# A rotary embedding on one core: six of eight rows of a tile worked in pairs, and the last tile stored as one transfer

## The chip, the cores and the metric

The kernel runs on one core of a Trainium2 chip. The metric is the device time of one execution in microseconds (us). Most executions of one kernel agree within 0.3%, so a difference of a tenth of a microsecond means nothing here. A run is called fast when it is not over 1.5% above the fastest of its kernel. Engines: PE is TensorE, PEld its weight loads, DVE VectorE, ACT ScalarE, POOL GpSimd, SP SyncE, whose queue issues all large transfers. In a profile page, a row of 40 digits gives the busy tenths of 40 equal slices of the span (9 is 90% or more), and the line of a DMA queue gives its packets, the MB moved and the share of the time of 16 DMA engines. The "span" is the profiled stretch of one execution; the device time is some 1.7 to 1.9 us longer.

## The reference

`x` has shape (16, 512, 1024) in fp32. Each row of 1024 is 16 heads of 64. Every head is split in halves `x1` and `x2` and rotated by tables that depend on the position in the sequence:

```python
x1, x2 = x[..., :half_dim], x[..., half_dim:]
rotated = concatenate([x1 * cos - x2 * sin, x1 * sin + x2 * cos], axis=-1)
```

So out = x * cos + swapped(x) * (-sin, sin): two products and one sum for each element, while 33.6 MB have to be read and as much written.

## The kernel before

The input is cut into 8 tiles of 128 partitions x 8 rows x 1024 numbers (4.2 MB each). The kernel keeps five tiles on the chip. The queue loads five tiles, stores tiles 0 to 2, loads tiles 5 to 7 into their places, and stores the rest. The results overwrite the tile.

```python
FIRST = (3, 8)        # tile 0 is loaded in two pieces
LAST_OUT = (4, 8)     # the last tile is stored in two halves
...
for t in range(NT):
    for k in range(KK):                       # eight rows of a tile
        r = xt[:, k * dim : (k + 1) * dim]
        own = k in DVE_B[t % 2]               # row 0
        if not own:                           # seven sine products on GpSimd
            b = bp.tile([P, dim], FP32, name="b")
            nc.gpsimd.tensor_tensor(out=halves(b), in0=swapped(r, nh), in1=over_heads(sk), op=ALU.mult)
        if k in PE_ROWS[t % 2]:               # rows 0 and 4: summed by TensorE, copied by ScalarE
            ...
        else:                                 # six rows: product and sum on VectorE
            add(1)
            ps = pd.tile([P, dim], FP32, name="pd")
            nc.vector.tensor_tensor(out=pairs(ps), in0=pairs(r), in1=cos_b(k, 2 * nh), op=ALU.mult)
            pending.append((r, ps, b))        # later: r = ps + b on VectorE
    ...
def finish(t):
    add(0)
    for hi in LAST_OUT if t == NT - 1 else (KK,):
        store(t, lo, hi)
```

## Time and profile before

| | before |
|---|---|
| device time | 162.39 us, median of 3 (162.34 to 162.41) |
| span | 160.7 us |
| VectorE busy | 141.4 us (88%) |
| GpSimd busy | 130.3 us (81%) |
| share of the DMA engines | 97.9% |
| moved | 67.24 MB, 432 GB/s from 10 to 150 us |

The prediction below shows the lines and reads them.

### The profile page before, as it was taken

The numbers are of one execution on the slowest core, as the hardware profiler recorded it, in microseconds if no ns is written. First come the engines' busy times: TensorE is split into PE (matmuls) and PEld (weight loads), VectorE is DVE, ScalarE is ACT, GpSimd is POOL, SyncE is SP. The second block draws the span as 40 slices with busy tenths as digits, with TensorE's granted clock in tenths as the row PEclk, the third lists the DMA queues.
The fourth block names the chain that finished last, engine by engine and source line by source line (L and its number), as shares of the span: only waits on it lengthen the run. The fifth ranks groups of instructions, "written<-read, shape, count | busy, mean of one in ns | idle before, by whom it ended". The sixth has DMA issues, their size and how long they took to land. (4 is left out here: it accounts for less than half of the span.)

```text
span 160.7 us, 531 instructions
## 1 busy us (share of the span) xinstructions
PE 62.1 (39%) x71; PEld 20.0 (12%) x71; DVE 141.4 (88%) x142; ACT 20.0 (12%) x33; POOL 130.3 (81%) x62
## 2 busy tenths in 40 slices
PE   3146370536217250709045540918063722735000
PEld 0112010202011110202020200211020201120000
DVE  1059999999999999999999999999999999999800
ACT  0201120021102020111102020202001110202000
POOL 1039999999999999999999899999999799940000
PEclk9999958576956776595555555555555585587655
DMA  5999999999999999999999999999999999999994
GB/s 190 398 408 473 392 490 424 392 481 432 392 432 473 394 432 473 400 400 498 408 400 465 441 400 434 457 416 424 465 408 424 473 408 416 465 416 412 416 432 192
DMA packets 2852, 67.26 MB, mean 419 GB/s; under 512 B 418, under 2 KB 546, under 8 KB 546
## 3 DMA queue, kind: packets, MB, share of 16 engines
q1 hardware_dynamic: 2752, 67.24, 97.9%
q10 hardware_dynamic: 98, 0.00, 0.0%
q14 instruction: 2, 0.02, 0.0%
HBM read 33.69 MB, written 33.55 MB: 419 GB/s over the span
## 5 line engine op out<-in xcount | busy, mean ns | idle before, releaser
L168 POOL TENSOR_TENSOR b<-xt,sns 128x1024 f32<-128x1024 f32 x56 | 129.6, 2354 | 11.6 <-DVE sns L111 9.2
L186 DVE TENSOR_TENSOR pd<-xt,tab 128x1024 f32<-128x1024 f32 x48 | 58.1, 1225 | 0.8
L148 DVE TENSOR_TENSOR xt<-pd,b 128x1024 f32<-128x1024 f32 x48 | 58.3, 1217 | 0.0
L181 PE MATMUL ps<-xt,ident 128*128 128x512 f32 x32 | 29.6, 1082 | 49.0 <-issue 38.4
L181 PE MATMUL ps<-b,ident 128*128 128x512 f32 x32 | 29.0, 1061 | 29.6 <-DVE ps L174 27.0
L182 ACT COPY xt<-ps 128x512 f32<-128x512 f32 x32 | 18.7, 585 | 120.4 <-PE ps L181 120.4
L174 DVE TENSOR_TENSOR ps<-xt,tab 128x512 f32<-128x512 f32 x32 | 20.6, 687 | 0.0
L181 PEld LDWEIGHTS ps<-xt,ident 128*128 128x128 f32 x32 | 9.4, 324 | 68.3 <-issue 63.7
L181 PEld LDWEIGHTS ps<-b,ident 128*128 128x128 f32 x32 | 9.2, 316 | 49.6 <-issue 25.6
L179 DVE TENSOR_TENSOR xt<-xt,tab 128x1024 f32<-128x1024 f32 x8 | 9.8, 1221 | 0.4
L110 DVE TENSOR_SCALAR sns<-tab 128x256 f32<-128x256 f32 x1 | 0.4, 425 | 8.1 <-PE tab L108 8.1
L107 PE MATMUL tab<-b,spread 64*128 64x256 f32 x2 | 1.2, 697 | 5.0 <-DMA b<-in_sin_dram 5.0
L182 ACT ACT_TABLE_LOAD x1 | 1.3, 1283 | 7.1 <-DMA xt<-in_x_dram 7.1
L97 PE MATMUL ps<-zero 128*128 128x512 bf16 x3 | 1.5, 623 | 1.2 <-DVE zero L94 1.2
L107 PEld LDWEIGHTS tab<-b,spread 64*128 64x128 f32 x2 | 0.5, 306 | 5.9 <-issue 5.9
L108 PE MATMUL tab<-b,spread 64*128 64x256 f32 x2 | 1.1, 632 | 0.0
L94 DVE MEMSET zero<- 128x256 uint32 x1 | 0.3, 272 | 0.9 <-PEq L211 0.9
L108 PEld LDWEIGHTS tab<-b,spread 64*128 64x128 f32 x2 | 0.7, 334 | 0.2
L106 DVE COPY spread<-ident 64x64 f32<-64x64 f32 x2 | 0.3, 182 | 0.2 <-POOL ident masks.py:199 0.2
L97 PEld LDWEIGHTS <-zero 128*128 128x128 bf16 x3 | 0.3, 124 | 1.5 <-DVE zero L94 1.2
masks.py:197 POOL MEMSET ident<- 128x128 f32 x1 | 0.2, 204 | 0.3 <-POOLq L211 0.3
L111 DVE COPY sns<-tab 128x256 f32<-128x256 f32 x1 | 0.4, 414 | 0.0
(6 smaller groups left out, 0.9 us busy)
## 6 DMA issues: line engine op xcount, KB each, us to landing
xt<-in_x_dram SPq DMA_DIRECT2D x7, 4096.0 KB, 29.1
out_dram<-xt SPq DMA_DIRECT2D x7, 4096.0 KB, 27.8
out_dram<-xt SPq DMA_DIRECT2D x2, 2048.0 KB, 8.4
xt<-in_x_dram SPq DMA_DIRECT2D x1, 2560.0 KB
xt<-in_x_dram SPq DMA_DIRECT2D x1, 1536.0 KB, 6.3
b<-in_sin_dram SPq DMA_DIRECT2D x1, 64.0 KB, 6.3
b<-in_cos_dram SPq DMA_DIRECT2D x1, 64.0 KB, 6.1
spare<-in_sin_dram ACTq DMA_DIRECT2D x1, 0.9 KB, 5.7
```

What stands on the lines that cost most here:

```text
L97: nc.tensor.matmul(out=ps, lhsT=zero[:, :P], rhs=zero, start=True, stop=True)
L107: nc.tensor.matmul(out=sin_t, lhsT=spread, rhs=sin_sb, start=True, stop=True)
L108: nc.tensor.matmul(out=cos_t, lhsT=spread, rhs=cos_sb, start=True, stop=True)
L110: nc.vector.tensor_scalar_mul(out=sns[:, :, 0, :], in0=sin_k, scalar1=-1.0)
L111: nc.vector.tensor_copy(out=sns[:, :, 1, :], in_=sin_k)
L148: nc.vector.tensor_tensor(out=r, in0=ps, in1=b, op=ALU.add)
L168: nc.gpsimd.tensor_tensor(out=halves(b), in0=swapped(r, nh), in1=over_heads(sk), op=ALU.mult)
L174: nc.vector.tensor_tensor(out=pairs(ps), in0=pairs(rc), in1=cos_b(k, BANK // half), op=ALU.mult)
L179: nc.vector.tensor_tensor(out=halves(r), in0=halves(r), in1=swapped_signed(k), op=ALU.mult)
L181: nc.tensor.matmul(out=ps, lhsT=ident, rhs=rhs, start=False, stop=True, skip_group_check=True)
L182: nc.scalar.copy(out=rc, in_=ps)
L186: nc.vector.tensor_tensor(out=pairs(ps), in0=pairs(r), in1=cos_b(k, 2 * nh), op=ALU.mult)
```

## The change

The intent is to save VectorE and GpSimd the fixed cost of instructions: six of the eight rows go in pairs, with one product and one sum of 2048 elements instead of two of 1024. Since the computation should then end earlier, the last tile is stored in one piece. Row 0 and row 3 (formerly 4) remain the ones that TensorE sums. The products of pairs have one buffer in PSUM (an on-chip memory) instead of two, and some tiny transfers differ as well.

```diff
-PE_ROWS = ((0, 4), (0, 4))
-DVE_B = ((0,), (0,))
+ROW_OWN, ROW_PE = 0, 3
+PAIRS = ((1, 2), (4, 5), (6, 7))
-LAST_OUT = (4, 8)
+LAST_OUT = (8,)
-SMALL = (15, 14, 12, 8)
+EXTRA = 5
...
-    bp = ctx.enter_context(tc.tile_pool(name="bp", bufs=B_BUFS))     # 6 of 1024
+    bp = ctx.enter_context(tc.tile_pool(name="bp", bufs=3))          # 3 of 2048
...
-    pd = ctx.enter_context(tc.tile_pool(name="pd", bufs=2, space=bass.MemoryType.PSUM))
+    pd = ctx.enter_context(tc.tile_pool(name="pd", bufs=1, space=bass.MemoryType.PSUM))
...
+    def pair_product(t, k):
+        ps = pd.tile([P, 2 * dim], FP32, name="pd")
+        cos_product(ps, rows(t, k, 2), k, 2)
+        return ps, rows(t, k, 2)
+    def pair_sum(ps, r, b):
+        nc.vector.tensor_tensor(out=r, in0=ps, in1=b, op=ALU.add)
...
+    for t in range(NT):
+        b1 = sin_rows(t, first[0], 2)        # GpSimd
+        p1 = pair_product(t, first[0])       # VectorE
+        own_product(r0)
+        ...
+        b3 = sin_rows(t, ROW_PE, 1)
+        b2 = sin_rows(t, second[0], 2)
+        pair_sum(*p1, b1)
+        pe_half(ROW_PE, *h0)
+        p2 = pair_product(t, second[0])
+        b1 = sin_rows(t, third[0], 2)
+        pair_sum(*p2, b2)
+        pe_half(ROW_PE, *h1)
+        p1 = pair_product(t, third[0])
+        if t + 1 < NT:
+            cos_product(own_ps, rows(t + 1, ROW_OWN), ROW_OWN)
+        pair_sum(*p1, b1)
+        stores(t)
```

(`+        ...` stands for TensorE's sum of row 0.)

More of the change, by code (lines that the diff above doesn't have):

```diff
@@ L14 @@
 BUFS = 5
-B_BUFS = 6
 BANK = 512
-PE_ROWS = ((0, 4), (0, 4))
-DVE_B = ((0,), (0,))
+ROW_OWN, ROW_PE = 0, 3
+PAIRS = ((1, 2), (4, 5), (6, 7))
 FIRST = (3, 8)
-LAST_OUT = (4, 8)
-SMALL = (15, 14, 12, 8)
+LAST_OUT = (8,)
+EXTRA = 5
 @with_exitstack
@@ L61 @@
     xp = ctx.enter_context(tc.tile_pool(name="xp", bufs=BUFS))
-    bp = ctx.enter_context(tc.tile_pool(name="bp", bufs=B_BUFS))
+    bp = ctx.enter_context(tc.tile_pool(name="bp", bufs=3))
     pfix = ctx.enter_context(tc.tile_pool(name="pfix", bufs=1, space=bass.MemoryType.PSUM))
-    pe = ctx.enter_context(tc.tile_pool(name="pe", bufs=3, space=bass.MemoryType.PSUM))
-    pd = ctx.enter_context(tc.tile_pool(name="pd", bufs=2, space=bass.MemoryType.PSUM))
+    pe = ctx.enter_context(tc.tile_pool(name="pe", bufs=1, space=bass.MemoryType.PSUM))
+    pd = ctx.enter_context(tc.tile_pool(name="pd", bufs=1, space=bass.MemoryType.PSUM))
     ctx.enter_context(tc.manual_schedule())
@@ L81 @@
     load(0, 0, FIRST[0])
-    sin_sb = bp.tile([P, dim], FP32, name="b")[:PB, : KK * half]
-    cos_sb = bp.tile([P, dim], FP32, name="b")[:PB, : KK * half]
+    tabs = bp.tile([P, 2 * dim], FP32, name="b")
+    sin_sb = tabs[:PB, : KK * half]
+    cos_sb = tabs[:PB, dim : dim + KK * half]
     nc.sync.dma_start(out=sin_sb, in_=sin_v)
@@ L89 @@
         load(t)
+    spare = fixed.tile([1, EXTRA, 16], FP32)
+    for i in range(EXTRA):
+        nc.sync.dma_start(out=spare[:1, i], in_=sin_v[:1, :16])
     ident = fixed.tile([P, P], FP32)
@@ L94 @@
     nc.vector.memset(zero, 0.0)
-    for i in range(3):
-        ps = pe.tile([P, BANK], FP32, name="ps")
+    own_ps = pe.tile([P, dim], FP32)
+    pe_ps = pe.tile([P, BANK], FP32)
+    for ps in (own_ps[:, :BANK], own_ps[:, BANK:], pe_ps):
         nc.tensor.matmul(out=ps, lhsT=zero[:, :P], rhs=zero, start=True, stop=True)
-    spare = fixed.tile([16, len(SMALL), 16], FP32)
     sns = fixed.tile([P, KK, 2, half], FP32)
@@ L104 @@
     spread = fixed.tile([PB, P], FP32)
-    for b in range(NB):
-        nc.vector.tensor_copy(out=spread[:, b * PB : (b + 1) * PB], in_=ident[:PB, :PB])
+    eye = ident[:PB, :PB]
+    nc.vector.tensor_copy(
+        out=spread.rearrange("p (b q) -> p b q", b=NB),
+        in_=bass.AP(tensor=eye.tensor, offset=eye.offset, ap=[eye.ap[0], [0, NB], [1, PB]]),
+    )
     nc.tensor.matmul(out=sin_t, lhsT=spread, rhs=sin_sb, start=True, stop=True)
@@ L111 @@
     nc.vector.tensor_copy(out=sns[:, :, 1, :], in_=sin_k)
-    on_dve = sorted(set(DVE_B[0]) | set(DVE_B[1]))
-    sns_t = tab[:, KK * half : KK * half + len(on_dve) * hd]
-    for i, k in enumerate(on_dve):
-        nc.vector.tensor_copy(out=sns_t[:, i * hd : (i + 1) * hd], in_=sns[:, k])
-    def cos_b(k, n):
-        c = cos_t[:, k * half : (k + 1) * half]
-        return bass.AP(tensor=c.tensor, offset=c.offset, ap=[c.ap[0], [0, n], [1, half]])
-    def over_heads(s):
-        return bass.AP(tensor=s.tensor, offset=s.offset, ap=[s.ap[0], [0, nh], [1, hd]])
@@ L124, in swapped @@
-    def swapped(r, n):
-        return bass.AP(
-            tensor=r.tensor, offset=r.offset + half, ap=[r.ap[0], [hd, n], [-half, 2], [1, half]]
-        )
-    def swapped_signed(k):
-        i = on_dve.index(k)
-        s = sns_t[:, i * hd : (i + 1) * hd]
-        return bass.AP(
-            tensor=s.tensor, offset=s.offset + half, ap=[s.ap[0], [0, nh], [-half, 2], [1, half]]
-        )
-    def pairs(r):
-        return r.rearrange("p (a j) -> p a j", j=half)
-    def halves(r):
-        return r.rearrange("p (h a j) -> p h a j", a=2, j=half)
@@ L143, with heads, swapped @@
-    pending = []
-    def add(most):
-        while len(pending) > most:
-            r, ps, b = pending.pop(0)
-            nc.vector.tensor_tensor(out=r, in0=ps, in1=b, op=ALU.add)
-    def finish(t):
-        add(0)
+    own_t = tab[:, KK * half : KK * half + hd]
+    nc.vector.tensor_copy(out=own_t, in_=sns[:, ROW_OWN])
+    def heads(r):
+        return r.rearrange("p (h a j) -> p h a j", a=2, j=half)
+    def swapped(r):
+        n = r.shape[1] // hd
+        return bass.AP(tensor=r.tensor, offset=r.offset + half, ap=[r.ap[0], [hd, n], [-half, 2], [1, half]])
@@ new lines, in rows, with cos_product @@
+    def rows(t, k, n=1):
+        return tiles[t][:, k * dim : (k + n) * dim]
+    def cos_product(out, r, k, n=1):
+        c = cos_t[:, k * half : (k + n) * half]
+        m = r.shape[1] // (n * half)
+        if n == 1:
+            cb = bass.AP(tensor=c.tensor, offset=c.offset, ap=[c.ap[0], [0, m], [1, half]])
+            o, i = (z.rearrange("p (a j) -> p a j", j=half) for z in (out, r))
+        else:
+            cb = bass.AP(tensor=c.tensor, offset=c.offset, ap=[c.ap[0], [half, n], [0, m], [1, half]])
+            o, i = (z.rearrange("p (k a j) -> p k a j", k=n, j=half) for z in (out, r))
+        nc.vector.tensor_tensor(out=o, in0=i, in1=cb, op=ALU.mult)
@@ new lines, in own_product, with sin_product @@
+    def own_product(r):
+        s = bass.AP(
+            tensor=own_t.tensor,
+            offset=own_t.offset + half,
+            ap=[own_t.ap[0], [0, nh], [-half, 2], [1, half]],
+        )
+        nc.vector.tensor_tensor(out=heads(r), in0=heads(r), in1=s, op=ALU.mult)
+    def sin_product(out, r, k, n):
+        s = sns[:, k : k + n].rearrange("p k a j -> p (k a j)")
+        if n == 1:
+            sb = bass.AP(tensor=s.tensor, offset=s.offset, ap=[s.ap[0], [0, nh], [1, hd]])
+            o, i = heads(out), swapped(r)
+        else:
+            sb = bass.AP(tensor=s.tensor, offset=s.offset, ap=[s.ap[0], [hd, n], [0, nh], [1, hd]])
+            o = out.rearrange("p (k h a j) -> p k h a j", k=n, a=2, j=half)
+            i = bass.AP(
+                tensor=r.tensor,
+                offset=r.offset + half,
+                ap=[r.ap[0], [dim, n], [hd, nh], [-half, 2], [1, half]],
+            )
+        nc.gpsimd.tensor_tensor(out=o, in0=i, in1=sb, op=ALU.mult)
@@ new lines, in sin_rows, with parts, pe_add, pe_half @@
+    def sin_rows(t, k, n):
+        b = bp.tile([P, 2 * dim], FP32, name="b")[:, : n * dim]
+        sin_product(b, rows(t, k, n), k, n)
+        return b
+    def parts(r):
+        return [r[:, i * BANK : (i + 1) * BANK] for i in range(r.shape[1] // BANK)]
+    def pe_add(ps, other):
+        nc.tensor.matmul(out=ps, lhsT=ident, rhs=other, start=False, stop=True, skip_group_check=True)
+    def pe_half(k, r, b):
+        cos_product(pe_ps, r, k)
+        pe_add(pe_ps, b)
+        nc.scalar.copy(out=r, in_=pe_ps)
@@ L152, in finish, with stores @@
+    def pair_product(t, k):
[4 more added lines that the diff above has]
+        nc.vector.tensor_tensor(out=r, in0=ps, in1=b, op=ALU.add)
+    def stores(t):
         lo = 0
@@ L158, in finish @@
                 load(n)
+    cos_product(own_ps, rows(0, ROW_OWN), ROW_OWN)
     for t in range(NT):
-        xt = tiles[t]
-        for k in range(KK):
-            r = xt[:, k * dim : (k + 1) * dim]
-            own = k in DVE_B[t % 2]
-            if not own:
-                b = bp.tile([P, dim], FP32, name="b")
-                sk = sns[:, k].rearrange("p a j -> p (a j)")
-                nc.gpsimd.tensor_tensor(out=halves(b), in0=swapped(r, nh), in1=over_heads(sk), op=ALU.mult)
-            if k in PE_ROWS[t % 2]:
-                parts = []
-                for c in range(0, dim, BANK):
-                    ps = pe.tile([P, BANK], FP32, name="ps")
-                    rc = r[:, c : c + BANK]
-                    nc.vector.tensor_tensor(
-                        out=pairs(ps), in0=pairs(rc), in1=cos_b(k, BANK // half), op=ALU.mult
-                    )
-                    parts.append((ps, rc, swapped(rc, BANK // hd) if own else b[:, c : c + BANK]))
-                if own:
-                    nc.vector.tensor_tensor(out=halves(r), in0=halves(r), in1=swapped_signed(k), op=ALU.mult)
-                for ps, rc, rhs in parts:
-                    nc.tensor.matmul(out=ps, lhsT=ident, rhs=rhs, start=False, stop=True, skip_group_check=True)
-                    nc.scalar.copy(out=rc, in_=ps)
-            else:
-                add(1)
-                ps = pd.tile([P, dim], FP32, name="pd")
-                nc.vector.tensor_tensor(out=pairs(ps), in0=pairs(r), in1=cos_b(k, 2 * nh), op=ALU.mult)
-                pending.append((r, ps, b))
-            if k == 0 and t > 0:
-                finish(t - 1)
-            add(1)
@@ L191 @@
-        if t == NT // 2 - 1:
-            for i, n in enumerate(SMALL):
-                nc.scalar.dma_start(out=spare[:n, i], in_=sin_v[:n, :16])
-    finish(NT - 1)
+        first, second, third = PAIRS
+        b1 = sin_rows(t, first[0], 2)
+        p1 = pair_product(t, first[0])
+        r0 = rows(t, ROW_OWN)
+        own_product(r0)
+        for ps, r in zip(parts(own_ps), parts(r0)):
+            pe_add(ps, swapped(r))
+        nc.scalar.copy(out=r0, in_=own_ps)
+        b3 = sin_rows(t, ROW_PE, 1)
@@ L198 @@
+        b2 = sin_rows(t, second[0], 2)
+        pair_sum(*p1, b1)
+        h0, h1 = zip(parts(rows(t, ROW_PE)), parts(b3))
+        pe_half(ROW_PE, *h0)
[8 more added lines that the diff above has]
+        stores(t)
 _INS = ['x', 'cos', 'sin', 'num_heads']
```

## The prediction

> **What bounds the kernel now.** I read first the page's busy shares and slices, then the table of DMA queues.
>
> ```profile
> PE 62.1 (39%) x71; PEld 20.0 (12%) x71; DVE 141.4 (88%) x142; ACT 20.0 (12%) x33; POOL 130.3 (81%) x62
> ...
> DVE  1059999999999999999999999999999999999800
> ACT  0201120021102020111102020202001110202000
> POOL 1039999999999999999999899999999799940000
> ...
> DMA  5999999999999999999999999999999999999994
> ...
> q1 hardware_dynamic: 2752, 67.24, 97.9%
> ```
>
> Three resources look full: VectorE (DVE), GpSimd (POOL) and the 16 DMA engines. What tells them apart is the edges. VectorE is idle in the first two slices and stops two slices before the end; the DMA row is full from the second slice to the last but one. The queue row says the same: 97.9% of 16 engines' span. So transfers bound the kernel, and VectorE matters only through when it releases stores. Next I cut the trace into windows (columns after the length: busy time of PE, PEld, DVE, ACT, POOL, then granted clock, DMA share, GB/s).
>
> ```profile
> 10.00:150.00 140.00, 58.64 (x64) 18.57 (x64) 138.68 (x138) 18.73 (x32) 129.60 (x56) 0.65 1.00 432
> 157.00:157.50 0.50, 0.00 (x0) 0.00 (x0) 0.00 (x0) 0.00 (x0) 0.00 (x0) 0.50 0.84 360
> 157.50:158.00 0.50, 0.00 (x0) 0.00 (x0) 0.00 (x0) 0.00 (x0) 0.00 (x0) 0.50 0.92 393
> 158.00:158.50 0.50, 0.00 (x0) 0.00 (x0) 0.00 (x0) 0.00 (x0) 0.00 (x0) 0.50 0.77 328
> 158.50:159.00 0.50, 0.00 (x0) 0.00 (x0) 0.00 (x0) 0.00 (x0) 0.00 (x0) 0.50 0.16 66
> ```
>
> From 10 to 150 us the DMA share is 1.00 at 432 GB/s: no hole. So a 4096 KB tile (4.194 MB) takes 4.194/432 = 9.7 us, and the engines run dry at about 158.5 us, the last of them a little later. Then the timeline of the end, and of the queue's own issues:
>
> ```profile
> 0.73 0.38 SPq L75 DMA_DIRECT2D xt<-in_x_dram  x1
> ...
> 147.14 1.22 DVE L148 TENSOR_TENSOR xt<-pd,b 128x1024 f32<-128x1024 f32 x1
> 148.39 1.23 DVE L186 TENSOR_TENSOR pd<-xt,tab 128x1024 f32<-128x1024 f32 x1
> 149.53 2.35 DVE L148 TENSOR_TENSOR xt<-pd,b 128x1024 f32<-128x1024 f32 x2
> ...
> 146.04 6.25 SPq L79 DMA_DIRECT2D out_dram<-xt  x2
> ```
>
> Computation ends at 149.53 + 2.35 = 151.88 us, the last half tile's store is issued at once (the issues end at 146.04 + 6.25 = 152.29), and its 2.1 MB need 4.9 us of the engines. Since they run dry at 158.5, they had earlier work until 153.6: the last half store joined a queue that was not yet empty. Today VectorE is some 1.6 us early at the only place where it could matter. The chain of waits ends in VectorE work, but that is the order of releases, not the limit.
>
> **What the Trainium skill says.**
> 1. "VectorE: DVE Perf Modes", section on the TRN2 errata: an fp32 tensor_tensor of N elements takes (N+151)/0.96 ns, exact at 512 and 2048. That is 691 and 1224 ns for 512 and 1024; the trace has 687, and 1217 to 1225. It agrees, so I use 2.29 us at 2048.
> 2. "GPSIMD Engine Reference", 3.1: a tensor_tensor of 2048 fp32 elements took 4497 ns. The trace shows only 1024 elements, 2354 ns; two of those are 4.71, so the pair would save 0.2 us of fixed cost. I use 4.5.
> 3. "DMA: Bandwidth & Descriptors", latency: about 0.6 us to the first byte for transfers issued by SyncE. This trace shows more: first load issued at 0.73 us, nothing moved before 1.7. I use 1.0.
> 4. "Perfetto Trace Analysis", DMA Optimizations: splitting a transfer lets parts start sooner. The change undoes such a split, so that is the part to fear.
>
> **The change part by part.**
>
> The lines for the operations concerned:
>
> ```profile
> L168 POOL TENSOR_TENSOR b<-xt,sns 128x1024 f32<-128x1024 f32 x56 | 129.6, 2354 | 11.6 <-DVE sns L111 9.2
> L186 DVE TENSOR_TENSOR pd<-xt,tab 128x1024 f32<-128x1024 f32 x48 | 58.1, 1225 | 0.8
> L148 DVE TENSOR_TENSOR xt<-pd,b 128x1024 f32<-128x1024 f32 x48 | 58.3, 1217 | 0.0
> ...
> L174 DVE TENSOR_TENSOR ps<-xt,tab 128x512 f32<-128x512 f32 x32 | 20.6, 687 | 0.0
> ...
> L179 DVE TENSOR_TENSOR xt<-xt,tab 128x1024 f32<-128x1024 f32 x8 | 9.8, 1221 | 0.4
> ```
>
> *VectorE.* A tile has 17 instructions now (6 + 6 + 4 + 1) and 10 afterwards: three products and three sums of 2048, two products of 512, and two of 1024. Elements stay equal: 15 x 1024. What counts is start to start. The timeline gives 149.53 - 148.39 = 1.14 us behind an instruction whose result is not awaited, and 148.39 - 147.14 = 1.25 behind one that is. With 1024 more elements at 1/0.96 ns: 2.20 and 2.32. For 512 it is 0.60. Afterwards a tile has two direct dependences (the second sum on its product, the next tile's first product on the one product buffer): 6 x 2.20 + 2 x 1.14 + 2 x 0.60 + 2 x 0.11 = 16.9 us. Now it is (151.88 - 10.75)/8 = 17.6. Saved: 0.7 us a tile.
>
> *GpSimd.* Per tile three of 4.5 and one of 2.35: 15.9 us, below VectorE's 16.9; now seven times 2.35 less overlap. It stays second, except in the first tile. There GpSimd starts at 10.54 and delivers the first pair at 15.0, the single row at 17.4 and the second pair at 21.9. VectorE from 10.75: 1.14 + 2.20 + 1.14 = 15.2, sum 17.4, half row 18.0, product 20.2; then it waits 1.7 us for the second pair. Sum 24.1, half row 24.7, product 26.9, next tile's first product 28.1, sum 30.3. GpSimd's third pair is there at 26.4, and its lead grows afterwards. The three buffers of b are freed in time: the third pair reuses the first pair's, free at 17.4.
>
> *End of computation.* 30.3 + 7 x 16.9 - 1.1 (no next tile) = 147.5 us, against 151.9 now. So 4.4 us earlier, all beside the transfers.
>
> *The last store.* It is now 9.7 us of transfer issued at once. The engines have nothing else from 158.5 - 9.7 = 148.8 us on. To reach them in time it has to be issued by 148.8 - 1.0 = 147.8. It is issued at about 147.5 to 147.6. So the early end of computation is spent, nearly to the last tenth, on the coarser store. The latest engine has a little more slack than the mean one, and it is the latest that sets the end.
>
> *The rest.* The order of large transfers is the same. Store 0 moreover waits for load 2 (a shared DMA semaphore). Five loads occupy the engines to about 52 us, and load 2 has landed by about 34, so nothing runs dry. The five tiny transfers replace four tiny ones (49 rows); the latter have 0.0% of the queue table. PE and ACT have the same matmuls and elements, and the own row's copy is one of 1024; both are idle over half the time.
>
> Sum: transfers unchanged, expected bubble before the last store 0 to 0.3 us. Time 162.4 plus 0.1: **162.5 us**.
>
> **Rivals.**
> A. *The coarse last store opens a hole.* For it: the margin above is 0.3 us out of an estimate over eight tiles; 0.1 us a tile of error moves it by 0.8. Against it: 512, 1024 and the skill's 2048 lie on one line. If VectorE were as slow as now, the issue would be at 151.9, 4.1 us late: 166.5 us (slower by 2.5%). With half the saving: about 164.5.
> B. *GpSimd becomes the bound.* For it: the pair product walks one dimension more, and GpSimd has under 1.1 us of slack a tile. Against it: its present product already swaps halves and runs steadily at 2342 to 2368 ns. At 5% more it just matches VectorE; at 15% more, 18.3 us a tile, computation would end near 157 and the time be 171 or so.
> C. *The saved VectorE work shows in the time.* For it: VectorE is 88% busy and lies on the chain of waits. Against it: the 1.00 DMA share from 10 to 150 us. It would need DMA holes, and there are none; were it true, 4.4 us less: 158.
> D. *Two transfers' worth of smoother DMA*, fewer and larger packets at the end or other tiny transfers: some tenths either way.
>
> **Range and chances.** My centre has no hole or a small one. The upper end allows 1.2 us of hole, the lower end some tenths of better DMA: 162.0 to 163.6. Slower by 2% means over 165.6, a hole of 3.2 us, possible only if A is nearly whole or B is true: 0.05. Faster needs C: 0.01. Within 2%: 0.94.
>
> **What would show it.** In the profile afterwards: DMA share about 98% and the same GB/s; VectorE instructions of 2048 at 2.28 to 2.30 us, GpSimd's at 4.45 to 4.6; VectorE waiting for GpSimd some 1.7 us in tile 0 and hardly later; computation ending near 147.5; the last store issued then and landing about 12 us later; DMA share under 1 for at most some tenths around 148 to 149. Wrong would be: pair instructions longer than twice the single ones, GpSimd busy without pause and VectorE waiting in each tile, or a hole in the DMA row before the last store.

## The result, and the profile after

The changed kernel took 162.38 us (median of 4, 162.19 to 162.47), the kernel before in the same rounds 162.40 us (162.34 to 162.44). The ratio is 0.9997, 95% interval 0.998 to 1.0015: the same. A ratio here is always the mean time of one kernel's fast runs over that of the other's fast runs of the same rounds, so it is not quite the ratio of the medians.

The page of the changed kernel, the lines that answer to those shown of before:

```profile
PE 56.4 (35%) x71; PEld 18.8 (12%) x71; DVE 136.3 (85%) x85; ACT 18.1 (11%) x25; POOL 127.2 (79%) x38
...
DVE  1059969999999999999999999999999999998000
POOL 1049999999999999988998899898999899840000
...
DMA  5999999999999999999999999999999999999993
...
q1 hardware_dynamic: 2618, 67.24, 97.9%
```

VectorE has 57 instructions fewer and 5.1 us less busy time, and its row ends one slice (4 us) earlier. The DMA row and the queue's 97.9% have not moved. From 10 to 150 us the windows give 432 GB/s in both kernels. The large transfers are the same, and so is the time.

The groups by shape (busy us and mean ns of one, then the idle time before them and who ended it) show the costs of the paired instructions:

```profile
L165 POOL TENSOR_TENSOR b<-xt,sns 128x2048 f32<-128x2048 f32 x24 | 108.4, 4530 | 14.5 <-DVE sns L117 9.1 <-DVE xt L189 5.4
L141 DVE TENSOR_TENSOR pd<-xt,tab 128x2048 f32<-128x2048 f32 x24 | 55.0, 2291 | 0.2
L189 DVE TENSOR_TENSOR xt<-pd,b 128x2048 f32<-128x2048 f32 x24 | 54.9, 2287 | 2.4 <-POOL b L165 1.6
```

A pair costs VectorE 2.29 us, where two single instructions cost 2 x 1.22 = 2.44, and GpSimd 4.53, where two cost 4.71. VectorE waits for GpSimd once, 1.6 us in the first tile; GpSimd waits 5.4 us in all for VectorE to free buffers. So GpSimd is the second of the two, not the first.

The end of the computation in the timeline (start, duration), and the issue of the last store:

```profile
138.21 2.29 DVE L141 TENSOR_TENSOR pd<-xt,tab 128x2048 f32<-128x2048 f32 x1
...
140.60 2.29 DVE L189 TENSOR_TENSOR xt<-pd,b 128x2048 f32<-128x2048 f32 x1
...
143.40 2.29 DVE L141 TENSOR_TENSOR pd<-xt,tab 128x2048 f32<-128x2048 f32 x1
...
145.80 2.29 DVE L189 TENSOR_TENSOR xt<-pd,b 128x2048 f32<-128x2048 f32 x1
...
148.15 0.33 SPq L78 DMA_DIRECT2D out_dram<-xt  x1
```

VectorE ends at 148.09 us instead of 151.88, so 3.8 us earlier. The single store leaves at 148.15 us. In the packet records of this run, ten of the sixteen DMA engines have a hole of 0.08 to 0.55 us at about 149 us, before the first packet of the last store; the others had earlier work until then. Fifteen engines end between 158.74 and 158.99 us. The sixteenth has no hole and ends at 159.51: it was late anyway, and it is the one that the end waits for. In the kernel before, the ends lie between 158.32 and 159.38. The early end of computation has thus been spent on the coarser store.

### The profile page after: what moved, and what is told of

Same layout as the page of the kernel before. It is cut to its first block, busy times and chain, and to the rows that moved or that the text cites. A ratio compares the mean times of both kernels' runs of the same rounds, so it can differ in the third digit from the quotient of the medians.

```text
span 160.7 us, 443 instructions
## 1 busy us (share of the span) xinstructions
PE 56.4 (35%) x71; PEld 18.8 (12%) x71; DVE 136.3 (85%) x85; ACT 18.1 (11%) x25; POOL 127.2 (79%) x38
## 3 DMA queue, kind: packets, MB, share of 16 engines
q1 hardware_dynamic: 2618, 67.24, 97.9%
## 4 chain that ended last, share of the span: by engine, by line
DVE 68%; issue 12%; POOL 6%; DMA 4%; PE 1%; SPq 0%; DVEq 0%
DVE xt L189 33%; DVE pd L141 31%; POOL b L165 6%; DMA b<-in_sin_dram 4%; DVE pe_ps L141 3%; PE tab L113 1%; PE tab L114 1%; DVE sns L116 0%; DVE xt L150 0%; DVE own_ps L141 0%; SPq L74 0%; DVE sns L117 0%; DVEq L189 0%
## 5 line engine op out<-in xcount | busy, mean ns | idle before, releaser
L165 POOL TENSOR_TENSOR b<-xt,sns 128x2048 f32<-128x2048 f32 (+1 forms) x32 | 126.5, 3987 | 14.5 <-DVE sns L117 9.1
L189 DVE TENSOR_TENSOR xt<-pd,b 128x2048 f32<-128x2048 f32 x24 | 54.9, 2287 | 2.4 <-POOL b L165 1.6
L141 DVE TENSOR_TENSOR pd<-xt,tab 128x2048 f32<-128x2048 f32 x24 | 55.0, 2291 | 0.2
L176 PE MATMUL own_ps<-xt,ident 128*128 128x512 f32 x32 | 29.1, 1064 | 54.0 <-DVE xt L150 48.3
L176 PE MATMUL pe_ps<-b,ident 128*128 128x512 f32 x32 | 25.2, 880 | 29.1 <-DVE pe_ps L141 29.1
L176 PEld LDWEIGHTS own_ps<-xt,ident 128*128 128x128 f32 x32 | 9.4, 324 | 74.0 <-DVE xt L150 59.3
L209 ACT COPY xt<-own_ps 128x1024 f32<-128x1024 f32 x8 | 8.1, 1013 | 72.2 <-PE own_ps L176 72.2
L181 ACT COPY xt<-pe_ps 128x512 f32<-128x512 f32 x16 | 9.4, 589 | 40.7 <-PE pe_ps L176 40.7
L141 DVE TENSOR_TENSOR pe_ps<-xt,tab 128x512 f32<-128x512 f32 x16 | 11.0, 686 | 0.0
L141 DVE TENSOR_TENSOR own_ps<-xt,tab 128x1024 f32<-128x1024 f32 x8 | 9.8, 1223 | 0.0
```

The lines of the kernel that those rows point to most:

```text
L141: nc.vector.tensor_tensor(out=o, in0=i, in1=cb, op=ALU.mult)
L165: nc.gpsimd.tensor_tensor(out=o, in0=i, in1=sb, op=ALU.mult)
L176: nc.tensor.matmul(out=ps, lhsT=ident, rhs=other, start=False, stop=True, skip_group_check=True)
L181: nc.scalar.copy(out=r, in_=pe_ps)
L189: nc.vector.tensor_tensor(out=r, in0=ps, in1=b, op=ALU.add)
L209: nc.scalar.copy(out=r0, in_=own_ps)
```

## Experiments

My theory: the DMA engines set the time. The computation has only to release the last store before the queue runs dry, the single store moved that deadline 4 to 5 us forward, and the pairs moved the computation forward by nearly as much. The rivals: the pairs do gain time and the single store eats exactly that (so undoing the store should show 158.5 us); the single store costs nothing by itself; VectorE or the computation's traffic still governs the time.

Each experiment is an edit of the changed kernel unless it says otherwise. Results are correct except in the one without computation. Each kernel before in these rounds had a median of 162.34 to 162.38 us.

### The four combinations

**The changed kernel again**, as a yardstick.

> The changed kernel once more, as the yardstick beside the next three on the same chip. Theory (the DMA engines set the time, the computation only has to release the last store by about 148 us): 162.2 to 162.5 us, ratio to the kernel before within 0.2% of 1; computation ends at 148.1 and most engines have a hole of 0.1 to 0.6 us before the last store, hidden behind the one engine that is latest anyway. Rival (VectorE's shorter work shows in the time and something else takes it back): no different time, so this run alone does not tell them apart.

Measured: 162.37 us (162.25 to 162.46, 5 runs), ratio 0.9998 (0.9985 to 1.0012). VectorE ended at 147.88 us in its profile, and holes stood on five engines only (0.07 to 0.29 us). The latest engine again had no hole and ended at 159.41. As expected.

**Pairs, with the last store in halves again.**

```diff
-LAST_OUT = (8,)
+LAST_OUT = (4, 8)
```

> Pairs as in the change, but the last tile stored in two halves as before. Theory: the holes of 0.1 to 0.6 us at 149 us vanish (the second half is needed only at about 152.8 and is issued at 148.2), but the time moves by no more than 0.3 us: 162.1 to 162.4, same. Rival (the pairs gain 4 us and the single store costs 4 us, so they cancel): with the split store back, the gain shows, about 158.5 us.

Measured: 162.52 us (162.16 to 162.61, 5 runs), ratio 1.0004 (0.9991 to 1.0016). The gain that the rival wanted, 4 us, does not appear, although VectorE ends at 148.55 us and nothing is coarse any more. The median lies 0.1 us above the stated 162.1 to 162.4, which is within the scatter. The packet records show no hole on any engine around the last store, as expected. The pairs by themselves are worth nothing here. ("Pairs" stands for all of the change but the last store, the tiny transfers included; these were not tested apart.)

**Single rows, with the last store in one piece** (an edit of the kernel before).

```diff
-LAST_OUT = (4, 8)
+LAST_OUT = (8,)
```

> Single rows as in the kernel before, but the last tile stored as one transfer. Theory: the store is issued at 151.9 to 152.0, its first bytes move 1.0 us later, at 152.9, while the engines have run dry between 148.6 and 149.7; so a hole of 3 to 4 us on each of them, no more hidden by the latest one, and 165.7 to 166.3 us (slower by 2.0 to 2.4%). Rival (a store of one piece costs nothing, as it is hidden anyway): 162.4.

Measured: 165.88 us (165.65 to 166.04, 4 runs), ratio 1.0214 (1.02 to 1.0228): 3.5 us slower. VectorE ends at 152.19. The queue's timeline and the windows (length, busy time by engine, clock, then DMA share and GB/s):

```profile
152.26 0.33 SPq L79 DMA_DIRECT2D out_dram<-xt  x1
```

```profile
149.00:150.00 1.00, 0.00 (x0) 0.00 (x0) 1.00 (x2) 0.00 (x0) 0.00 (x0) 0.50 0.00 0
...
152.00:153.00 1.00, 0.00 (x0) 0.00 (x0) 0.20 (x1) 0.00 (x0) 0.00 (x0) 0.50 0.00 0
153.00:154.00 1.00, 0.00 (x0) 0.00 (x0) 0.00 (x0) 0.00 (x0) 0.00 (x0) 0.50 1.22 524
```

No packet starts from 149 to 153 us, on any engine, while VectorE (the third busy time) works on the last rows: the hole that the paired kernel just avoids. The last packets of earlier work end between 148.6 and 149.5, and the first of the store start at 153.10. So the coarse store is not free, and the shorter computation is exactly what pays for it.

**No computation at all.** Loads and stores keep their order and sizes.

```diff
-    cos_product(own_ps, rows(0, ROW_OWN), ROW_OWN)
     for t in range(NT):
-        first, second, third = PAIRS
-        ...
         stores(t)
```

> The same loads and stores in the same order and sizes, and no rows computed at all: each store waits for its load alone. The result is wrong on purpose. Theory: the transfers alone take as long, 162.0 to 162.5 us, without holes at the last store. Rival 1 (computation slows the transfers, by its traffic to the on-chip memory or through late releases): clearly less, under 161 us. Rival 2 (it is VectorE that sets the time): far less, under 150.

Measured: 161.81 us (161.69 to 162.1, 5 runs), ratio 0.9968 (0.9955 to 0.998).

```profile
DMA  6999999999999999999999999999999999999995
...
q1 hardware_dynamic: 2618, 67.24, 98.3%
```

The transfers alone take as long, to 0.3%. That decides against both rivals: neither VectorE nor the traffic of the computation is what the time consists of. But 161.81 lies below my range of 162.0 to 162.5, and the interval excludes 1: some 0.5 us do come with the computation. In the profile the latest engine ends at 158.74 us, against 159.41 in the changed kernel, and one 8 KB transfer of instructions that the other has is missing. No run tests which of these it is, so it stays open. The packet records speak for the instructions: in nine of the ten runs of paired rows that show such a transfer (the changed kernel's own run and nine of the experiments), the latest engine's lag behind the median of the sixteen grows by 0.3 to 0.5 us within the very tile transfer during which the 8 KB come (79.77 us in the changed kernel, for 0.31 us). In the run with the early delay they come at 82.11 us, and the step comes one tile transfer later. In the tenth run (pairs, halves) another engine takes the step, and without computation there is none. The run also bounds what is to be had: with this order of transfers, no better computation can gain more than about 0.3%.

### How sharp is the deadline?

I delayed VectorE by a known amount: the last pair product of the last tile is written twice, or four times, to the same place with the same values.

```diff
         p1 = pair_product(t, third[0])
+        for _ in range(1 if t == NT - 1 else 0):      # 3 for the longer delay
+            cos_product(p1[0], p1[1], third[0], 2)
```

With the store in one piece:

> The changed kernel with the last pair product of the last tile done twice: 2.2 to 2.3 us more on VectorE just before the last sum, result right. Theory: the single last store is issued at 150.4 instead of 148.15, its bytes start at 151.4 and end 9.7 to 9.8 us later; the time is 1.6 to 2.1 us longer than the changed kernel's, 164.0 to 164.5. Rival (there is slack left before the last store): 162.4.

> The same with the last pair product done four times: 6.6 to 6.9 us more. Theory: past the threshold each us costs one us, so 4.4 to 4.6 us more than with one repetition: 168.4 to 169.1 us. Rival (slack): less than half of that.

Measured: 164.12 us (163.95 to 164.33, 4 runs), ratio 1.011 (1.0095 to 1.0126), and 168.85 us (168.59 to 168.95, 4 runs), ratio 1.0399 (1.0383 to 1.0414). VectorE ended at 150.18 and 155.05 us. The page and the queue's timeline of the longer delay:

```profile
DMA  5999999898999989898999999898999999950885
...
q1 hardware_dynamic: 2618, 67.24, 94.2%
```

```profile
155.12 0.33 SPq L78 DMA_DIRECT2D out_dram<-xt  x1
```

The row has an empty slice just before the last three, as it also had in the run of single rows with one store. From one delay to the other VectorE ended 4.87 us later and the time grew by 4.73. Past the deadline one microsecond costs one.

With the store in halves, the same two delays:

> Pairs with the last tile stored in halves, and 2.2 to 2.3 us more on VectorE in front of the last sum. Theory: the second half is issued at 150.4 and needed only by about 152.8, so the delay is hidden: 162.1 to 162.5. Rival (any delay of the last store counts): 164.5.

> The same with 6.6 to 6.9 us more. Theory: the second half is issued at 154.8 to 155.0, 2.0 to 2.2 us too late: 164.1 to 164.7 us. Rival (any delay counts): 169.

Measured: 162.25 us (162.21 to 162.47, 4 runs), ratio 0.9998 (0.9981 to 1.0015), and 163.99 us (163.94 to 164.27, 4 runs), ratio 1.0105 (1.009 to 1.012). VectorE ended at 150.29 and 155.00. The first delay is hidden whole, the second but for 1.7 us. That is a little less than the 2.0 to 2.2 us that I expected, so 163.99 lies 0.1 us below my range of 164.1 to 164.7; "any delay counts" is refuted all the same. By this one point, the split store lets the computation end nearly 5 us later at the same time.

### Is there slack in between, and can the first tile's wait be won back?

**The delay in the third tile** instead of the last:

```diff
+        for _ in range(1 if t == 2 else 0):
+            cos_product(p1[0], p1[1], third[0], 2)
```

> The changed kernel with the doubled product in the third tile instead of the last, five tiles before the end. Theory: VectorE has no slack in between, it works without a pause from the second tile on, so the delay arrives whole at the last store: VectorE ends at 150.2 to 150.5 and the time is 163.9 to 164.3, as with the late delay. Rival (waits further on absorb it): 162.4.

Measured: 164.11 us (163.91 to 164.3, 4 runs), ratio 1.0093 (1.004 to 1.0145). VectorE ended at 150.36, and the time is that of the late delay (164.12). Nothing on the way absorbs it, as VectorE has no waits after the first tile.

**The first tile reordered.** GpSimd computes the second pair before the single row, and VectorE takes the single row later, in the first tile only.

(The edit, shortened.)

```diff
-        b3 = sin_rows(t, ROW_PE, 1)
-        b2 = sin_rows(t, second[0], 2)
+        if t == 0: b2 = sin_rows(t, second[0], 2); b3 = sin_rows(t, ROW_PE, 1)
+        else:      b3 = sin_rows(t, ROW_PE, 1); b2 = sin_rows(t, second[0], 2)
...        # in tile 0, half h0 comes after the second sum and h1 before the third
```

> The changed kernel, but in the first tile GpSimd computes the second pair before the single row, and VectorE takes the single row's halves later, so that the wait of 1.6 us for the second pair goes. Estimate from the trace: some 0.5 us of new waits, so VectorE ends 1.0 to 1.4 us earlier, at 146.7 to 147.1, and the holes before the last store vanish. Theory (the transfers set the time): no gain beyond 0.2 us, 162.2 to 162.5. Rival (VectorE's end still sets the time): 161.0 to 161.4.

Measured: 162.21 us (162.16 to 162.29, 4 runs). The ratio of 0.9977 has a wide interval, 0.9934 to 1.002, because one run of the kernel before in these rounds took 163.78 us, so I read the medians. VectorE's waits and its last sum:

```profile
DVE xt L189 <- POOL b L165: 0.2, 1, 0.2
```

```profile
144.68 2.29 DVE L189 TENSOR_TENSOR xt<-pd,b 128x2048 f32<-128x2048 f32 x1
```

The wait is 0.2 us instead of 1.6, and VectorE ends at 146.97, 1.1 us earlier than in the changed kernel. No packet record shows a hole before the last store. The time does not move beyond the noise.

**The same, with the late delay of 2.3 us:**

> The same with the last pair product of the last tile done twice (2.3 us more just before the last sum). Theory: it ends at 149.0 to 149.4, first bytes 0.9 us later, so the time lies 1.0 to 1.4 us below that of the same delay without the reordering (164.1): 162.7 to 163.1. Rival (the reordering buys nothing there either): 164.1.

Measured: 162.98 us (162.85 to 163.54, 4 runs), ratio 1.0031 (0.9985 to 1.0077). VectorE ended at 149.09, 1.09 us earlier than with the same delay and no reordering, and the time is 1.14 us shorter. So the reordering's microsecond is real; it is worthless only while the deadline is met.

The ten experiments with computation together (end of VectorE in the profiled run, median time):

| kernel | last store | VectorE ends | time | time minus end |
|---|---|---|---|---|
| first tile reordered | one | 146.97 | 162.21 | 15.2 |
| changed kernel again | one | 147.88 | 162.37 | 14.5 |
| reordered, late by 2.3 | one | 149.09 | 162.98 | 13.9 |
| late by 2.3 | one | 150.18 | 164.12 | 13.9 |
| early delay | one | 150.36 | 164.11 | 13.8 |
| single rows | one | 152.19 | 165.88 | 13.7 |
| late by 6.9 | one | 155.05 | 168.85 | 13.8 |
| pairs | halves | 148.55 | 162.52 | 14.0 |
| late by 2.3 | halves | 150.29 | 162.25 | 12.0 |
| late by 6.9 | halves | 155.00 | 163.99 | 9.0 |

With one store the time is the end plus 13.8 us, or 162.3, whichever is more. The deadline is thus at 162.3 - 13.8 = 148.5 us, and the changed kernel meets it with about half a microsecond to spare. With halves the one point past it gives 162.3 - 9.0 = 153.3. No version beat both kernels, and the run without computation says that there is hardly anything left to beat them by.

## Why the prediction was right

The predicted 162.5 us, range 162.0 to 163.6, holds 162.38. Step by step:

- **What bounds the kernel.** Right, and shown: the transfers without computation take 161.81 us.
- **Instruction costs.** VectorE 2.287 and 2.291 us (I had used 2.29), GpSimd 4.530 (4.5). The wait in the first tile was 1.57 us (1.7), the only one of VectorE for GpSimd; rival B fell.
- **A tile's period.** Predicted 16.9 us; from the first product of tile 1 (30.23) to that of tile 7 (132.08) it is 101.85/6 = 16.98. The term that was mis-sized is the second sum behind its own product: 140.60 - 138.21 = 2.39 us instead of 2.32. That is some 0.08 us a tile, 0.45 over the six tiles. In the last tile I also overlooked a dependence: with no next tile's product in between, the third sum follows its own product at once (145.80 - 143.40 = 2.40 us instead of 2.20). Together they are the 0.6 us by which computation ended later than I said, 148.09 instead of 147.5.
- **The margin before the last store.** The mechanism was right and three sizes were off, in opposite directions. Computation ended 0.6 us later. The first packets follow the issue by 0.8 us (153.10 - 152.26 and 155.94 - 155.12 in the two runs with a dry queue), not 1.0. And the engines run dry at 158.7 us on average by the packet records of before, not at 158.5, as I had taken packets to end where the windows count their start. So the mean engine needed the issue by 158.7 - 9.7 - 0.8 = 148.2, and it came at 148.15: no margin on the mean engine, small holes on ten, and none on the latest, which sets the end. That the latest engine has more slack, I had said. That the later end of computation met a deadline that was itself 0.4 us later than I had worked out was luck: with the end as it was and the deadline at 147.8, the mean engine would have had a hole of some 0.3 us.
- **How early VectorE was before.** I said 1.6 us, the last half store being needed from 153.6 on. That leaves out the latency of an issue, which I did subtract for the single store: with my own 1.0 us it was 0.6. By the delays of the split store, where the latest engine counts and not the mean one, it was 153.3 - 151.88 = 1.4.
- **Store 0.** It did wait for load 2: it was issued at 33.20 us, though its last sum had ended at 30.19. It cost nothing that the DMA row shows.
- **Rival A, sized.** I said 166.5 us for a VectorE that ends at 151.9. The combination of single rows and one store shows 165.88 at 152.19: it cost 3.5 us instead of 4.1. The latency was shorter, and the latest engine ran dry later than the mean: its hole in the packet records is some 3.7 us long (149.46 to about 153.2), that of the earliest some 4.5.
- **Rival D.** Larger packets at the end gained nothing to be seen: pairs took 162.37 us with one store and 162.52 with halves, and the ranges of the runs overlap. The tiny transfers were not tested apart.
- **Rival C.** The saved VectorE work did not show as time in any run whose last store was in time.
- **What I proposed to look for.** One check was blunt: "DMA share under 1 for some tenths around 148 to 149". The window from 148 to 149 us has 0.46 in the changed kernel and 0.62 before, where no hole was; only the packet records, or holes of whole microseconds, can be read there.

## What to carry to other kernels

When the transfer engines are full from edge to edge, as here, a shorter computation is no gain by itself; it is slack, and the only place where it was seen to count in this kernel is the release of the last store before the queue runs dry. Work out that deadline (end of transfers, minus the duration of the last store, minus the latency of an issue) before coarsening the last store: here 4 us of saved VectorE work paid for it with half a microsecond left, and without the saving it cost 3.5 us. A repeated, harmless instruction is a cheap probe of whether an engine lies before or behind such a deadline.

## What the Trainium skill lacked or had wrong

- "DMA: Bandwidth & Descriptors", Latency and other measured facts: it gives about 0.6 us to the first byte for transfers issued by SyncE. It does not say from which moment it counts. Here the first packet record starts 0.82 and 0.84 us after the issue begins when the queue is dry, which is 0.49 and 0.51 us after the issue of 0.33 us ends; at the start of the kernel it is 1.02 us after the beginning (0.73 to 1.75) and 0.64 after the end. A deadline for an issue needs the figure from the beginning.
- The same page, Where 436 GB/s comes from: it says without a condition that for transfers between HBM and the chip's memory the HBM side, about 358 GB/s, binds. In this program on one core it did not: 432 GB/s, reads and writes together, held for 140 us, close to the 435 that it names as the fabric's ceiling. The same page's measured table, 425 GB/s for a core alone and about 358 with both cores of a pair at work, agrees with the run; the sentence lacks that condition.
- "VectorE: DVE Perf Modes", the TRN2 errata: the formula for one fp32 tensor_tensor, (N+151)/0.96 ns, gives 2291 ns at 2048 and the trace has 2287 to 2291. What a chain of them costs is the spacing of starts, which this formula does not give: 2.20 us where the next does not depend on the last, 2.32 for a product into the buffer that the sum before it has just read, and 2.39 for a sum that reads the product written just before it in PSUM. The same section's table has 58 + FD cycles (FD: elements of one partition) for a VectorE instruction, with the remark that this is too little for a single one. It does not say that this row fits the spacing: at its 0.96 GHz it gives, as an estimate, 2194, 1127 and 594 ns for 2048, 1024 and 512, and the independent starts here lie 2.20, 1.13 to 1.14 and 0.60 us apart.
- "GPSIMD Engine Reference", 3.1: it has an add of 2048 elements alone, at 4497 ns. The product with swapped halves took 4530, so the figure carries over to this access pattern within 1%.
